# Two-layer HGRN2 and attention trunk: forget and query products moved ahead of v, attention scores taken eight heads at a time, and both groups of the recurrence in the same visits

## The chip, the cores and the metric

The kernel runs on one core of a Trainium2 chip. The metric is the time of one execution on the device in microseconds (us). A core has five engines that work beside each other: TensorE (PE in the profile, its weight loads PEld), VectorE (DVE), ScalarE (ACT), GpSimd (POOL) and SyncE (SP, which issues the loads here). Products go from SBUF through TensorE into PSUM, eight banks of 128 x 512 fp32, and only VectorE and ScalarE take them from there.

## The reference

256 tokens of width 1024 go through two layers. Each layer takes one wide projection of the normalised input, runs two mixers on parts of it, merges them through gates, and ends in a feed-forward of hidden width 2816. Cut to what matters:

```python
for l in range(2):
    h = rmsnorm(x, norm1[l])
    hq, hf, hi, hg, aq, ak, av, ga, gb = split_cols(h @ w_in[l])
    q = silu(hq)                                   # 8 heads of 128
    f = lb + (1 - lb) * sigmoid(hf)                # decay per token and channel
    k = 1 - f
    # linear recurrence with state S of 128 x 128 per head:
    #   S_t = diag(f_t) S_(t-1) + k_t v_t^T,  o_t = q_t S_t     (v = hi)
    o = hgrn2_chunked(q, k, hi, log(max(f, 1e-30)))
    y_a = (rmsnorm(o, hg_norm[l]) * silu(hg)) @ w_pa[l]
    # 16 query heads of 64 on 4 key heads, window 128, partial rope, sinks
    y_b = swa_with_sinks(rope(aq), rope(ak), av, attn_sinks[l]) @ w_pb[l]
    x = x + (sigmoid(ga) * y_a + sigmoid(gb) * y_b) @ w_o[l]
    h2 = rmsnorm(x, norm2[l])
    x = x + (silu(h2 @ w_gate[l]) * (h2 @ w_up[l])) @ w_down[l]
return rmsnorm(x, final_norm)
```

## The kernel before

**The stream.** Nearly all of TensorE's time is a stream of wide products. Each weight is split into a high part `wh` (ACT casts it, `high`) and a low part `wl` (DVE subtracts, `low`), and each product is taken three times, high by high, high by low and low by high. A unit is 128 x 1024 weights. `form_a` spends 12 products of 512 columns on one and yields after every six, `form_b` (which leaves its result transposed, tiles `pb` for hf and hq) spends eight of 512 and eight of 256 columns on one and yields after every eight. One such yield is called a step below. There are five buffers for `wh` and five for `wl` (`NW`): `used()`, called when a unit is spent, prepares the unit four further on, so the vector engines are at most about four units ahead of TensorE. SP loads weights in the order of `plan`, 1 MB at a time, into three buffers.

**The order of a layer.** `layer` goes through ak and av (one product, `akv`), aq, v (16 steps), pb (32 steps: f and q of heads 0 to 3, group 0, then of heads 4 to 7, group 1), gate (16 steps), gb, yb, gb, yb, ga, ga (8 steps each), ya, wo, and then the feed-forward. The rest of a layer are side generators: `run` counts the steps of the stream and lets each side continue after as many steps as it asked for in its last yield. What a side has TensorE do at one place is called a visit: small products between two steps of the stream. While `pe_order` is set, TensorE's instructions keep the order in which the program issues them; all others are put in order by the framework's planner, which works with its own costs.

**Attention** (`attention`, gaps `YN`, `YQ`, `YE`) starts with v. `queries` transposes q of eight heads. `attend(n)` takes the scores of four heads (tiles `qk`) into two banks tagged "at" and two tagged "hg"; DVE adds the mask and takes the maximum on the way out, ACT takes the exponentials and DVE divides. `turn(n)` transposes the weights (tiles `pt`), `values(n)` multiplies them with av (tiles `pv`), and its result is split into the pair `att` that yb reads. Counted in steps from the start of v: queries(0) at 6, scores 0 at 8 and 1 at 16, turn(0) at 20, queries(1) at 23, values 0 with scores 2 in one visit at 27, turn(1) at 31, values 1 with scores 3 at 38, turn(2) at 42, turn(3) at 53, and values 2 and 3 at 56.

**The recurrence** (`recurrence`, gaps `GAPS`) is done for each group by `decays` (sigmoids and the affine steps that make f, k and q) and `chain`, which doubles the length over which decays are multiplied together: pk (DVE), products `lb`, DVE, products `lc`, DVE, products `lv` of length 16, DVE, `lv` of length 32, DVE, `lv` of length 64 and the crossing `lx`, copies, output `o` (reads v), its norm, transposes `ot`, and the split into the pair `oT` that ya reads. Each yield of `chain` is followed by either TensorE's part or the vector part. `chain` of group 0 uses PSUM banks "hg" and the SBUF buffer "pk", group 1 "at" and "sp"; "sp" holds the scores before. Group 1 runs one stage behind group 0, so that a visit holds two different stages: lb of group 0 at step 61, lb1 with lc0 at 69, lc1 with lv16 of 0 at 82, lv16 of 1 with lv32 of 0 at 90, lv32 of 1 with lv64 and lx of 0 at 96, lv64 and lx of 1 with o of 0 at 102, o of 1 with ot of 0 at 109, ot of 1 at 115. ya begins at 112 with the half that needs group 0, and at 120 takes the half that needs group 1.

Of the kernel before, what the change touches and what calls it, by code (L numbers as in the profile page):

```python
# [15 lines left out]
P = 128  # L16
D = 1024
S = 256
# [9 lines left out]
EPS = 1e-6  # L28
MIN_F = 1e-30
NRAW, NW = 3, 5  # L30
YD, YE, YQ = 2, 3, 5
YN = (8,), (4, 3, 4), (4, 7), (4, 11)
GAPS = ((8,), (6, 7), (3, 5), (3, 3), (3, 3), (4, 3), (4, 2), (1,))
NEG = -1e30

C_HQ, C_HF, C_HI, C_HG, C_AQ, C_AK, C_GA, C_GB = 0, 1024, 2048, 3072, 4096, 5120, 5632, 6656
# [6 lines left out]
def trunk(ctx, tc, x, norm1, w_in, lb_logits, hg_norm, attn_sinks, w_pa, w_pb, w_o, norm2,  # L43
# [110 lines left out]
    plan = []  # L154
    for l in range(DEPTH):
        win = w_in[l]
        for c0 in (C_AK, C_AQ, C_AQ + 512, C_HI, C_HI + 512):
            plan += [(win, 0, 4, c0, 512), (win, 4, 4, c0, 512)]
        for g in range(2):
            for col in (C_HF, C_HQ):  # L160
                plan += [(win, 0, KT, col + 512 * g + 256 * b, 256) for b in range(2)]
        for c in range(2):
            plan += [(win, 0, 4, C_HG + 512 * c, 512), (win, 4, 4, C_HG + 512 * c, 512)]
        for c in range(2):
            plan += [(win, 0, 4, C_GB + 512 * c, 512), (win, 4, 4, C_GB + 512 * c, 512)] + a_chunk(w_pb[l], c)
        for c in range(2):
            plan += [(win, 0, 4, C_GA + 512 * c, 512), (win, 4, 4, C_GA + 512 * c, 512)]
        plan += [(w_pa[l], 4 * h, 4, 512 * c, 512) for h in range(2) for c in range(2)]
        plan += a_chunk(w_o[l], 0) + a_chunk(w_o[l], 1)
        for gi, (b0, nb) in enumerate(groups):  # L170
            for b in range(nb // 2):
                plan += [(w[l], 0, KT, (b0 + 2 * b) * P, 256) for w in (w_gate, w_up)]
            if gi:
                plan += [(w_down[l], groups[gi - 1][0], 4, 512 * c, 512) for c in range(2)]
        plan.append((w_down[l], groups[-1][0], 2, 0, D))
# [266 lines left out]
    def layer(l, n1):  # L442
# [35 lines left out]
        mix = [btile([P, D], f"mix{l}{t}") for t in range(NT)]  # L478
        gate = [btile([P, D], f"gate{l}{t}") for t in range(NT)]
        att = halves(f"att{l}")  # L480
        oT = halves(f"o{l}")
        mT = halves(f"m{l}", "rh")
        fqk = [[btile([P, 4, S], f"{n}{l}{g}", "h") for n in "fqk"] for g in range(2)]
        state = {}

        def keys():
            for t in range(NT):
# [13 lines left out]
                    T.transpose(ps[:, i * P:(i + 1) * P], aq[t][:, g * 512 + i * P:g * 512 + (i + 1) * P], ident)  # L501
                A.copy(qT[g][:, :, t * P:(t + 1) * P], ps.rearrange("p (i c) -> p i c", i=4))

        def attend(n):
            g, i0 = n // 2, 2 * (n % 2)
            s = state["sp"][:, n % 2]
            m = sm.tile([P, 4, 2, 2, 2], F32, tag="stat", name=f"stat{l}{n}", bufs=3)
            pss = [[psum(f"qk{l}{n}{t}{u}", "hg" if t else "at") for u in range(2)] for t in range(NT)]
            for t in range(NT):
                W = (t + 1) * P  # L510
                for i in range(2):
                    for u in range(2):
                        pr = slice(u * 64, u * 64 + 64)
                        T.matmul(pss[t][u][:, i * W:(i + 1) * W], qT[g][pr, i0 + i, t * P:(t + 1) * P], kT[pr, g, 0:W],
                                 start=True, stop=True)
            yield
            for t in range(NT):
                W = (t + 1) * P
                for i in range(2):
                    for u in range(2):  # L520
                        V.tensor_tensor_reduce(s[:, 2 * u + i, t * P:t * P + W], pss[t][u][:, i * W:(i + 1) * W],
                                               amask[:, 256 - W:256], op0=ALU.add, op1=ALU.max, scale=1.0,
                                               scalar=-3.0e38, accum_out=m[:, 0, t, u, i:i + 1])
            nsk = nsink.rearrange("p (l g u h) -> p l g u h", l=DEPTH, g=2, u=2)[:, l, g, :, i0:i0 + 2]
            for t in range(NT):
                V.scalar_tensor_tensor(m[:, 1, t], m[:, 0, t], -0.125, nsk, ALU.mult, ALU.min)
                V.tensor_tensor(m[:, 2, t], m[:, 1, t], nsk, ALU.subtract)
            for t in range(NT):
                for u in range(2):
                    for i in range(2):  # L530
                        sv = s[:, 2 * u + i, t * P:t * P + (t + 1) * P]
                        A.activation(sv, sv, AF.Exp, bias=m[:, 1, t, u, i:i + 1], scale=0.125,
                                     accum_out=m[:, 0, t, u, i:i + 1])
            state["exp"] = A.activation(m[:, 2], m[:, 2], AF.Exp).ins
            V.tensor_tensor(m[:, 3], m[:, 0], m[:, 2], ALU.add)
            V.reciprocal(m[:, 3], m[:, 3])
            for t in range(NT):
                for u in range(2):
                    for i in range(2):
                        sv = s[:, 2 * u + i, t * P:t * P + (t + 1) * P]  # L540
                        V.tensor_scalar(sv, sv, m[:, 3, t, u, i:i + 1], None, ALU.mult)

        def turn(n):
            s = state["sp"][:, n % 2]
            for u in range(2):
                ps = psum(f"pt{l}{n}{u}", "at")
                for i in range(2):
                    for t in range(NT):
                        T.transpose(ps[:, i * S + t * P:i * S + t * P + P], s[:, 2 * u + i, t * P:t * P + P], ident)
                A.copy(s[:, 2 * u:2 * u + 2, 0:S], ps.rearrange("p (i c) -> p i c", i=2))  # L550
            ps = psum(f"pt{l}{n}2", "hg")
            for i in range(4):
                T.transpose(ps[:, i * P:(i + 1) * P], s[:, i, 2 * P:3 * P], ident)
            A.copy(s[:, :, S:3 * P], ps.rearrange("p (i c) -> p i c", i=4))

        def values(n, bank):
            g, pT = n // 2, state["sp"][:, n % 2]
            po = psum(f"pv{l}{n}", bank)
            for u in range(2):
                vs = slice(256 + (2 * g + u) * HD, 256 + (2 * g + u + 1) * HD)  # L560
                for i in range(2):
                    o = po[i * 64:i * 64 + 64, u * S:(u + 1) * S]
                    T.matmul(o, akv[0][:, vs], pT[:, 2 * u + i, 0:S], start=True, stop=False)
                    T.matmul(o[:, P:S], akv[1][:, vs], pT[:, 2 * u + i, S:3 * P], start=False, stop=True)
            yield
            hi, lo = (a.rearrange("p (u n) c -> p n u c", u=2)[:, n % 2] for a in att[g])
            split(hi, lo, po.rearrange("p (u c) -> p u c", u=2))
# [8 lines left out]

        def attention():
            state["sp"] = sm.tile([P, 2, 4, 384], F32, tag="sp", name=f"sp{l}", bufs=1)
            for t in range(NT):
                rope(aq[t], QH, t)  # L580
            yield YQ
            queries(0)
            yield 2
            for n, gaps in enumerate(YN):
                visit = [values(n - 2, "mm")] if n > 1 else []
                together(*visit, attend(n))
                if n == 3:
                    state["last"] = True
                yield gaps[0]
                if n:  # L590
                    turn(n - 1)
                    yield gaps[1]
                if n == 1:
                    queries(1)
                    yield gaps[2]
            turn(3)
            yield YE
            together(values(2, "at"), values(3, "at"))
            yield 5

        def decays(g):
            f, q, k = fqk[g]
# [10 lines left out]
        def chain(g):  # L613
# [121 lines left out]
            for i in range(8):  # L735
                h, a = i // 2, i % 2 * P
                T.matmul(ps[0:64, i, :], k[:, h, a:a + 64], q[:, h, a + 64:a + P], start=True, stop=True)
            px = psum(f"lx{l}{g}", tag).rearrange("p (i c) -> p i c", c=P)
            for h in range(4):
                T.matmul(px[:, h, :], kx[:, h, :], qx[:, h, :], start=True, stop=True)  # L740
# [42 lines left out]
        def recurrence():  # L783
            while "last" not in state:
                yield 1
            for g in range(2):
                decays(g)
            yield YD
            chains = [chain(g) for g in range(2)]
            next(chains[0])  # L790
            yield 1
            while atd[0] is not None:
                yield 1
            for n, gaps in enumerate(GAPS):
                live = [c for g, c in enumerate(chains) if 0 <= n - g < len(GAPS) - 1]
                pe_order[0] = True
                for c in live[::-1]:
                    next(c)
                pe_order[0] = False
                for c, gap in zip(live, gaps):  # L800
                    next(c, None)
                    if n == 0:
                        next(chains[1])
                    yield gap

        yield from proj("akv", lambda t, ps: evac_scaled(akv[t], ps, rs[t]), skew=l > 0, late=None if l else rest)
# [7 lines left out]
            tables()  # L814
        finish(ksd)
        atd = start(attention(), 1)
        for c in range(2):
            yield from proj(f"v{c}", lambda t, ps: evac_scaled(v[t][:, c * 512:(c + 1) * 512], ps, rs[t]))
        for g in range(2):
            for dst in fqk[g][:2]:  # L820
                for b in range(2):
# [5 lines left out]
                        used()  # L827
                    V.tensor_tensor(dst[:, 2 * b:2 * b + 2], dst[:, 2 * b:2 * b + 2], rb, ALU.mult)
        rec = start(recurrence(), 1)

        def put_gate(c):
            def f_(t, ps):
# [331 lines left out]
```

## Time and profile before

| | |
|---|---|
| median of 3 runs | 933.36 us (932.88 to 933.45) |
| the profiled execution's own time | 933.17 us |
| its span, first to last instruction | 931.4 us |
| TensorE busy / weight loads | 923.1 us (99%) / 781.5 us |
| VectorE, ScalarE, GpSimd busy | 675.2, 540.8, 20.5 us |
| granted clock of TensorE | 0.998 of full |
| from HBM | 159.42 MB |

The span runs from the first to the last instruction; the profiled execution's own time holds 1.8 us more, before and after it. Busy times of the engines overlap. A matmul's row lasts longer than the time until the next one starts, since matmuls are pipelined; the price of a product is read from start to start.

### The profile page before, as it was taken

To read this page: it belongs to the slowest core of one execution; us is meant where nothing else is said; L and a number is where in the kernel's file an instruction comes from. 1 tells how busy PE (TensorE), PEld (TensorE's weight loads), DVE (VectorE), ACT (ScalarE), POOL (GpSimd) and SP (SyncE) were. 2 spreads that over 40 slices of the span, in tenths; PEclk is the share of its full clock that TensorE was granted. 3 is DMA by queue.
4 is the path that set the end of the run, shared out by engine and by line. 5 is a ranking of instruction groups with operands and counts; after the bars stand their busy time and mean duration, and the time that the engine had idled before them with its cause. 6 is when DMAs were issued, how large, how long until landed. Compare 5 with 4: busy or idle time off the path is not lost.

```text
span 931.4 us, 14391 instructions
## 1 busy us (share of the span) xinstructions
PE 923.1 (99%) x5726; PEld 781.5 (84%) x5726; DVE 675.2 (72%) x1171; ACT 540.8 (58%) x914; POOL 20.5 (2%) x31
## 2 busy tenths in 40 slices
PE   9999999999999999999999999999999999999997
PEld 7888888888888888888888888888888888888885
DVE  6667789975778766766865677898667777667665
ACT  6566795465456545545555867945554565555553
POOL 2000000001000000000000000000010000000000
PEclk9999999999999999999999999999999999999999
DMA  8735426644546655566465444545445565556531
GB/s 299 259 127 192 136 92 194 205 145 136 181 136 200 198 190 181 186 197 203 163 200 187 136 137 145 173 162 194 151 153 180 165 197 181 181 189 203 194 138 46
DMA packets 111395, 161.40 MB, mean 173 GB/s; under 512 B 2912, under 2 KB 64672, under 8 KB 111328
## 3 DMA queue, kind: packets, MB, share of 16 engines
q1 hardware_dynamic: 110848, 159.42, 52.5%
q8 instruction: 45, 0.74, 0.3%
q10 hardware_dynamic: 320, 0.79, 0.2%
q0 software_dynamic: 160, 0.26, 0.1%
q14 instruction: 22, 0.18, 0.1%
HBM read 159.42 MB, written 1.05 MB: 172 GB/s over the span
## 4 chain that ended last, share of the span: by engine, by line
PE 99%; DVE 0%; ACT 0%; POOL 0%; issue 0%; DVEq 0%; ACTq 0%; POOLq 0%
PE pg L57 13%; PE pu L57 13%; PE acc L57 13%; PE pb L57 10%; PE gate L57 5%; PE gb L57 5%; PE v L57 5%; PE yb L57 5%; PE wo L57 5%; PE ya L57 5%; PE ga L57 5%; PE aq L57 5%; PE akv L57 2%; PE qk L57 1%; PE pv L57 1%; PE o L57 1%
## 5 line engine op out<-in xcount | busy, mean ns | idle before, releaser
L57 DVE TENSOR_TENSOR wl<-raw,wh 128x1024 fp32r<-128x1024 f32 (+1 forms) x301 | 364.3, 1220 | 126.8 <-ACT wh L57 125.4
L57 ACT CAST wh<-raw 128x1024 fp32r<-128x1024 f32 (+1 forms) x301 | 314.5, 1050 | 168.5 <-PE acc L57 46.0
L57 PE MATMUL pu<-xx_n,wh 128*128 128x512 f32 x352 | 92.6, 393 | 0.0
L57 PE MATMUL pg<-xx_n,wh 128*128 128x512 f32 x352 | 92.1, 393 | 0.0
L57 PEld LDWEIGHTS pg<-xx_n,wh 128*128 128x128 f32 x352 | 63.2, 189 | 11.0
L57 PEld LDWEIGHTS pu<-xx_n,wh 128*128 128x128 f32 x352 | 63.1, 189 | 10.9
L57 PE MATMUL acc<-wh,ah 128*128 128x512 f32 x174 | 68.1, 391 | 0.0
L57 PE MATMUL acc<-wh,al 128*128 128x512 f32 x174 | 67.8, 390 | 0.0
L57 PE MATMUL acc<-wl,ah 128*128 128x512 f32 x174 | 67.8, 389 | 0.0
L57 PE MATMUL pb<-xx_n,wh 128*128 128x512 f32 x256 | 66.3, 396 | 0.0
L57 PEld LDWEIGHTS pb<-xx_n,wh 128*128 128x128 f32 x256 | 45.4, 189 | 8.9 <-DVE wl L57 0.7
L57 PEld LDWEIGHTS pg<-xx_n,wl 128*128 128x128 f32 x352 | 48.4, 190 | 4.1 <-ACT xx_n L57 0.6
L57 PEld LDWEIGHTS pu<-xx_n,wl 128*128 128x128 f32 x352 | 48.4, 191 | 3.6
L57 PE MATMUL pg<-xx_n,wl 128*128 128x256 f32 x352 | 50.3, 284 | 0.0
L57 PE MATMUL pu<-xx_n,wl 128*128 128x256 f32 x352 | 49.8, 283 | 0.0
L57 ACT COPY zg<-pg 128x256 f32<-128x256 f32 x44 | 16.4, 372 | 53.1 <-PE pg L57 53.1
L57 PE MATMUL gate<-wh,xx_n 128*128 128x512 f32 x128 | 41.5, 395 | 0.0
L57 ACT ACTIVATE sp<-sp,stat 128x128 f32<-128x128 f32 (+1 forms) x64 | 28.2, 442 | 22.5 <-DVE stat L57 22.5
L57 PE MATMUL gb<-wh,xx_n 128*128 128x512 f32 x128 | 41.2, 393 | 0.0
L57 PE MATMUL ga<-wh,xx_n 128*128 128x512 f32 x128 | 41.0, 394 | 0.0
L57 PE MATMUL v<-wh,xx_n 128*128 128x512 f32 x128 | 40.9, 394 | 0.0
L57 PE MATMUL aq<-wh,xx_n 128*128 128x512 f32 x128 | 40.3, 391 | 0.0
(247 smaller groups left out, 1671.2 us busy)
## 6 DMA issues: line engine op xcount, KB each, us to landing
raw<-in_w_in SPq DMA_DIRECT2D x58, 1024.0 KB, 5.2
raw<-in_w_gate SPq DMA_DIRECT2D x22, 1024.0 KB, 5.1
raw<-in_w_up SPq DMA_DIRECT2D x22, 1024.0 KB, 5.0
raw<-in_w_down SPq DMA_DIRECT2D x22, 1024.0 KB, 5.0
raw<-in_w_pb SPq DMA_DIRECT2D x8, 1024.0 KB, 5.1
raw<-in_w_pa SPq DMA_DIRECT2D x8, 1024.0 KB, 4.9
raw<-in_w_o SPq DMA_DIRECT2D x8, 1024.0 KB, 4.9
raw<-in_w_in SPq DMA_DIRECT2D x3, 512.0 KB, 7.4
```

Source lines behind the costliest of these rows:

```text
L57: ins = call(*args, **kw)
```

## The change

In `layer`, the projections of f and q (pb) come before those of v, in the order of `plan` and of the products. Attention still starts after aq, so it now runs beside pb and the first v steps.

`attend(g)` takes the scores of eight heads in one visit: the four of the first half share the "at" banks with the second half for the first token block, and their second token block goes to two "mm" banks, which the stream also uses. The exponentials of the halves follow one after the other. Scores of the third and fourth half lie in other buffers ("pk" and two new tiles tagged "r"), so that all four are kept until one visit takes all values. `turn` copies its third bank with two ACT instructions and not one.

`recurrence` calls `decays` for both groups three steps apart, starts `chain` only when attention has ended, and then lets both groups do the same stage in the same visit; `chain` has a yield more, between lv64 and lx, so that the visit of `LEV` takes lv64 of both groups and then lx of both.

Counted in steps from the start of pb, the visits are now: queries(0) at 6, queries(1) at 7, scores of eight heads at 9, turn(0) at 20, turn(1) at 24, scores of the other eight at 26, turn(2) at 37, turn(3) at 44, all values at 47; pk of group 0 at 48 and of group 1 at 51; then, each for both groups, lb at 54, lc at 66, lv16 at 78, lv32 at 88, lv64 and lx at 96, o at 102, ot at 108. v takes steps 32 to 48, gate 48 to 64, ya begins at 112 as before.

```diff
-YD, YE, YQ = 2, 3, 5
-YN = (8,), (4, 3, 4), (4, 7), (4, 11)
-GAPS = ((8,), (6, 7), (3, 5), (3, 3), (3, 3), (4, 3), (4, 2), (1,))
+YD, YE, YQ = 3, 1, 5
+YN = (6, 5, 4, 2), (6, 5, 7, 3)
+LEV = 3, 3
+GAPS = (6, 6), (6, 6), (5, 5), (4, 4), LEV, (4, 2), (1, 1)
...
-        for c0 in (C_AK, C_AQ, C_AQ + 512, C_HI, C_HI + 512):
+        for c0 in (C_AK, C_AQ, C_AQ + 512):
             plan += [(win, 0, 4, c0, 512), (win, 4, 4, c0, 512)]
         for g in range(2):
             for col in (C_HF, C_HQ):
                 plan += [(win, 0, KT, col + 512 * g + 256 * b, 256) for b in range(2)]
+        for c in range(2):
+            plan += [(win, 0, 4, C_HI + 512 * c, 512), (win, 4, 4, C_HI + 512 * c, 512)]
...
+        state = {"sr": [btile([P, 4, S], f"sr{l}{u}", "r") for u in range(2)]}
...
+        def score(n, u):
+            if n < 2:
+                return state["sp"][:, n, 2 * u:2 * u + 2]
+            return state["sq"][:, 2 * u:2 * u + 2] if n == 2 else state["sr"][u].rearrange(
+                "p a c -> p (a c)")[:, 0:768].rearrange("p (i c) -> p i c", i=2)
+
+        def attend(g):
+            t0 = [psum(f"qk{l}{g}0{u}", "at") for u in range(2)]
+            t1 = [[psum(f"qk{l}{g}1{i0}{u}", "hg" if i0 else "mm") for u in range(2)] for i0 in range(2)]
+            ms, pss = [], []
+            for i0 in range(2):
...
+                pss.append([[ps[:, i0 * S:i0 * S + S] for ps in t0], t1[i0]])
+                for t in range(NT):
...
+                            T.matmul(pss[i0][t][u][:, i * W:(i + 1) * W], qT[g][pr, 2 * i0 + i, t * P:(t + 1) * P],
+                                     kT[pr, g, 0:W], start=True, stop=True)
+            yield
+            for i0, (m, ps) in enumerate(zip(ms, pss)):
...
+                            V.tensor_tensor_reduce(score(2 * g + i0, u)[:, i, t * P:t * P + W],
...
+            for i0, m in enumerate(ms):
...
+                            A.activation(sv, sv, AF.Exp, bias=m[:, 1, t, u, i:i + 1], scale=0.125,
...
+                yield
...
-            A.copy(s[:, :, S:3 * P], ps.rearrange("p (i c) -> p i c", i=4))
+            for u in range(2):
+                A.copy(score(n, u)[:, :, S:3 * P], ps[:, u])
...
+            queries(0)
+            yield 1
+            queries(1)
             yield 2
+            for g, gaps in enumerate(YN):
+                it = attend(g)
+                together(it)
+                yield gaps[0]
+                next(it)
+                if g == 1:
                     state["last"] = True
+                yield gaps[1]
+                turn(2 * g)
+                yield gaps[2]
+                turn(2 * g + 1)
+                yield gaps[3]
+            together(*(values(n, ("at", "hg")[n % 2]) for n in range(4)))
             yield YE
...
                 T.matmul(ps[0:64, i, :], k[:, h, a:a + 64], q[:, h, a + 64:a + P], start=True, stop=True)
+            yield
             px = psum(f"lx{l}{g}", tag).rearrange("p (i c) -> p i c", c=P)
...
             for g in range(2):
                 decays(g)
-            yield YD
-            chains = [chain(g) for g in range(2)]
-            next(chains[0])
-            yield 1
+                yield YD
             while atd[0] is not None:
                 yield 1
-            for n, gaps in enumerate(GAPS):
-                live = [c for g, c in enumerate(chains) if 0 <= n - g < len(GAPS) - 1]
+            chains = [chain(g) for g in range(2)]
+            for c in chains:
+                next(c)
+                yield 3
+            for gaps in GAPS:
                 pe_order[0] = True
-                for c in live[::-1]:
-                    next(c)
+                for _ in range(1 + (gaps is LEV)):
+                    for c in chains:
+                        next(c)
                 pe_order[0] = False
-                for c, gap in zip(live, gaps):
+                for c, gap in zip(chains, gaps):
                     next(c, None)
-                    if n == 0:
-                        next(chains[1])
                     yield gap
...
         atd = start(attention(), 1)
-        for c in range(2):
-            yield from proj(f"v{c}", lambda t, ps: evac_scaled(v[t][:, c * 512:(c + 1) * 512], ps, rs[t]))
         for g in range(2):
...
         rec = start(recurrence(), 1)
+        for c in range(2):
+            yield from proj(f"v{c}", lambda t, ps: evac_scaled(v[t][:, c * 512:(c + 1) * 512], ps, rs[t]))
```

## Rows read from the trace of the kernel before

**Rows 1.** The page's first part (busy time, share of the span and instructions of each engine), and the view of waits for TensorE: who waited for whom, us in total, times, the longest.

```profile
PE 923.1 (99%) x5726; PEld 781.5 (84%) x5726; DVE 675.2 (72%) x1171; ACT 540.8 (58%) x914; POOL 20.5 (2%) x31
...
PE warm L57 <- POOL ident L57: 1.6, 1, 1.6
```

**Rows 2.** The chain that ended last, in order of time, in two stretches: start in us, us, what, how many instructions.

```profile
372.00 5.58 PE pg L57 x32
...
478.84 8.17 PE aq L57 x36
```

**Rows 3.** TensorE's timeline in the second layer around the visit of lb of group 0 and in the visit of lb of group 1 and lc of group 0: start, us, engine, line, operation, out<-in, rows*columns of the array, count.

```profile
605.01 0.39 PE L57 MATMUL gate<-wh,xx_n 128*128 128x512 f32 x1
605.33 1.31 PE L57 MATMUL lb<-pk,k 128*32 128x80 f32 x64
606.57 0.50 PE L57 MATMUL gate<-wh,xx_n 128*128 128x512 f32 x1
606.91 0.40 PE L57 MATMUL gate<-wl,xx_n 128*128 128x512 f32 x1
...
617.68 1.31 PE L57 MATMUL lb<-pk,k 128*32 128x80 f32 x64
618.81 0.86 PE L57 MATMUL lc<-p,k 128*32 128x48 f32 x64
```

**Rows 4.** The same view around three visits of attention: scores alone, values with scores, and values of two halves.

```profile
512.68 0.39 PE L57 MATMUL v<-wh,xx_n 128*128 128x512 f32 x1
513.00 1.58 PE L57 MATMUL qk<-kT,qT 64*128 64x128 f32 x16
...
514.85 0.40 PE L57 MATMUL v<-wl,xx_n 128*128 128x512 f32 x1
...
544.29 0.63 PE L57 MATMUL pb<-xx_n,wl 128*128 128x256 f32 x4
544.85 1.57 PE L57 MATMUL pv<-sp,akv 128*64 128x256 f32 x16
546.35 1.58 PE L57 MATMUL qk<-kT,qT 64*128 64x128 f32 x16
...
548.44 0.63 PE L57 MATMUL pb<-xx_n,wh 128*128 128x512 f32 x2
...
595.18 0.39 PE L57 MATMUL gate<-wh,xx_n 128*128 128x512 f32 x1
...
598.64 0.39 PE L57 MATMUL gate<-wl,xx_n 128*128 128x512 f32 x1
```

**Rows 5.** The same view at the beginning of the visit that holds lv64 and lx of group 1, and around the last transposes `ot`.

```profile
670.26 0.39 PE L57 MATMUL ga<-wh,xx_n 128*128 128x512 f32 x1
670.58 1.15 PE L57 MATMUL lv<-q,k 128*64 128x64 f32 x16
671.65 1.16 PE L57 MATMUL lx<-qx,kx 128*128 128x128 f32 x8
...
696.38 0.40 PE L57 MATMUL ya<-wh,o1l 128*128 128x512 f32 x1
...
697.72 0.39 PE L57 MATMUL ya<-wl,o1h 128*128 128x512 f32 x1
```

**Rows 6.** Windows of the second layer: v, pb, gate, and gb to the second yb. Columns: stretch, its length, busy us (and instructions) of PE, PEld, DVE, ACT, POOL, granted clock, DMA share, GB/s.

```profile
501.30:527.20 25.90, 25.90 (x137) 20.79 (x136) 17.07 (x49) 18.17 (x35) 0.00 (x0) 1.00 0.43 135
527.20:583.30 56.10, 56.10 (x365) 48.77 (x366) 42.48 (x129) 39.57 (x98) 0.00 (x0) 1.00 0.49 156
583.30:611.00 27.70, 27.70 (x206) 22.68 (x205) 24.18 (x38) 23.39 (x34) 0.00 (x0) 1.00 0.49 166
611.00:662.50 51.50, 51.50 (x601) 42.60 (x600) 46.90 (x81) 27.71 (x38) 0.00 (x0) 1.00 0.53 172
```

**Rows 7.** VectorE's timeline between the visits at 605.33 and 617.68.

```profile
605.17 1.24 DVE L57 TENSOR_TENSOR q<-pk,f 128x256 f32<-128x256 f32 x2
606.30 0.97 DVE L57 TENSOR_TENSOR pk<-pk,f 128x768 f32<-128x768 f32 x1
607.17 0.71 DVE L57 TENSOR_TENSOR f<-f 128x512 f32<-128x512 f32 x1
...
611.44 0.68 DVE L57 TENSOR_TENSOR pk<-pk,f 128x512 f32<-128x512 f32 x1
...
612.38 0.62 DVE L57 TENSOR_TENSOR pk<-pk,f 128x256 f32<-128x256 f32 x1
612.90 2.37 DVE L57 TENSOR_TENSOR wl<-raw,wh 128x1024 fp32r<-128x1024 f32 x2
615.17 1.41 DVE L57 SCALAR_TENSOR_TENSOR gate<-gate,r_n,gate 128x512 f32<-128x512 f32 x2
```

**Rows 8.** Three rows of timelines: a cast on ScalarE, a product on VectorE, and the beginning of the visit of lc of group 1 with lv16 of group 0 on TensorE.

```profile
604.08 1.05 ACT L57 CAST wh<-raw 128x1024 fp32r<-128x1024 f32 x1 [1.03 <-PE gate L57]
...
634.78 0.76 DVE L57 TENSOR_TENSOR q<-p,f 128x256 f32<-128x256 f32 x2
...
637.50 0.89 PE L57 MATMUL lc<-p,k 128*32 128x48 f32 x64
```

**Rows 9.** GpSimd's timeline in the second layer (the load that spreads the row of norms), and from the groups of instructions of VectorE between 501.3 and 583.3 the masked maximum of 256 columns: count | busy us, mean ns | idle before.

```profile
490.60 0.56 POOL L406 DMA_DIRECT2D rb_n<-row_n  x1 [1.62 <-ACT aq L57]
...
L57 DVE CUSTOM_DVE_ANT_0 sp<-qk,cf 128x256 f32<-128x256 f32 x16 | 5.8, 420 | 0.0
```

More of the change, by code (lines that the diff above doesn't have):

```diff
@@ L483, in layer @@
         fqk = [[btile([P, 4, S], f"{n}{l}{g}", "h") for n in "fqk"] for g in range(2)]
-        state = {}
         def keys():
@@ L502, in queries @@
                 A.copy(qT[g][:, :, t * P:(t + 1) * P], ps.rearrange("p (i c) -> p i c", i=4))
[L504 to L511, printed above, removed]
-                    for u in range(2):
[L513 to L519, printed above, removed]
-                    for u in range(2):
[L521 to L541, printed above, removed]
@@ new lines, in score @@
+        def score(n, u):
[8 more added lines that the diff above has]
+            for i0 in range(2):
+                ms.append(sm.tile([P, 4, 2, 2, 2], F32, tag="stat", name=f"stat{l}{2 * g + i0}", bufs=3))
+                pss.append([[ps[:, i0 * S:i0 * S + S] for ps in t0], t1[i0]])
+                for t in range(NT):
+                    W = (t + 1) * P
+                    for i in range(2):
+                        for u in range(2):
+                            pr = slice(u * 64, u * 64 + 64)
+                            T.matmul(pss[i0][t][u][:, i * W:(i + 1) * W], qT[g][pr, 2 * i0 + i, t * P:(t + 1) * P],
+                                     kT[pr, g, 0:W], start=True, stop=True)
+            yield
+            for i0, (m, ps) in enumerate(zip(ms, pss)):
+                for t in range(NT)[::-1]:
+                    W = (t + 1) * P
+                    for u in range(2):
+                        for i in range(2):
+                            V.tensor_tensor_reduce(score(2 * g + i0, u)[:, i, t * P:t * P + W],
+                                                   ps[t][u][:, i * W:(i + 1) * W], amask[:, 256 - W:256],
+                                                   op0=ALU.add, op1=ALU.max, scale=1.0, scalar=-3.0e38,
+                                                   accum_out=m[:, 0, t, u, i:i + 1])
+            for i0, m in enumerate(ms):
+                n = 2 * g + i0
+                nsk = nsink.rearrange("p (l g u h) -> p l g u h", l=DEPTH, g=2, u=2)[:, l, g, :, 2 * i0:2 * i0 + 2]
+                for t in range(NT):
+                    V.scalar_tensor_tensor(m[:, 1, t], m[:, 0, t], -0.125, nsk, ALU.mult, ALU.min)
+                    V.tensor_tensor(m[:, 2, t], m[:, 1, t], nsk, ALU.subtract)
+                for t in range(NT):
+                    for u in range(2):
+                        for i in range(2):
+                            sv = score(n, u)[:, i, t * P:t * P + (t + 1) * P]
+                            A.activation(sv, sv, AF.Exp, bias=m[:, 1, t, u, i:i + 1], scale=0.125,
+                                         accum_out=m[:, 0, t, u, i:i + 1])
+                state["exp"] = A.activation(m[:, 2], m[:, 2], AF.Exp).ins
+                V.tensor_tensor(m[:, 3], m[:, 0], m[:, 2], ALU.add)
+                V.reciprocal(m[:, 3], m[:, 3])
+                for t in range(NT):
+                    for u in range(2):
+                        for i in range(2):
+                            sv = score(n, u)[:, i, t * P:t * P + (t + 1) * P]
+                            V.tensor_scalar(sv, sv, m[:, 3, t, u, i:i + 1], None, ALU.mult)
+                yield
@@ L543, in turn @@
         def turn(n):
-            s = state["sp"][:, n % 2]
             for u in range(2):
@@ L548, in turn @@
                     for t in range(NT):
[L549 to L553, printed above, removed]
-            A.copy(s[:, :, S:3 * P], ps.rearrange("p (i c) -> p i c", i=4))
+                        T.transpose(ps[:, i * S + t * P:i * S + t * P + P], score(n, u)[:, i, t * P:t * P + P], ident)
+                A.copy(score(n, u)[:, :, 0:S], ps.rearrange("p (i c) -> p i c", i=2))
+            ps = psum(f"pt{l}{n}2", "hg").rearrange("p (u i c) -> p u i c", u=2, i=2)
+            for u in range(2):
+                for i in range(2):
+                    T.transpose(ps[:, u, i], score(n, u)[:, i, 2 * P:3 * P], ident)
+            for u in range(2):
+                A.copy(score(n, u)[:, :, S:3 * P], ps[:, u])
         def values(n, bank):
-            g, pT = n // 2, state["sp"][:, n % 2]
+            g = n // 2
             po = psum(f"pv{l}{n}", bank)
@@ L562, in values @@
                     o = po[i * 64:i * 64 + 64, u * S:(u + 1) * S]
-                    T.matmul(o, akv[0][:, vs], pT[:, 2 * u + i, 0:S], start=True, stop=False)
-                    T.matmul(o[:, P:S], akv[1][:, vs], pT[:, 2 * u + i, S:3 * P], start=False, stop=True)
+                    T.matmul(o, akv[0][:, vs], score(n, u)[:, i, 0:S], start=True, stop=False)
+                    T.matmul(o[:, P:S], akv[1][:, vs], score(n, u)[:, i, S:3 * P], start=False, stop=True)
             yield
@@ L578, in attention @@
             state["sp"] = sm.tile([P, 2, 4, 384], F32, tag="sp", name=f"sp{l}", bufs=1)
+            state["sq"] = sm.tile([P, 4, 384], F32, tag="pk", name=f"sq{l}", bufs=1)
             for t in range(NT):
@@ L582, in attention @@
             queries(0)
+            yield 1
+            queries(1)
             yield 2
[L584 to L587, printed above, removed]
-                    state["last"] = True
[L589 to L596, printed above, removed]
+            for g, gaps in enumerate(YN):
[4 more added lines that the diff above has]
+                if g == 1:
+                    state["last"] = True
+                yield gaps[1]
[4 more added lines that the diff above has]
+            together(*(values(n, ("at", "hg")[n % 2]) for n in range(4)))
             yield YE
-            together(values(2, "at"), values(3, "at"))
-            yield 5
         def decays(g):
```

## The prediction

> **What bounds the kernel now.** First the page's busy times and the waits of TensorE: 923.1 us busy in a span of 931.4, and one wait, 1.6 us at the start [rows 1]. The reader is to see that no other engine ever makes TensorE wait, so that the time is a sum of TensorE's products. Then the chain that ended last, for the price of the stream: 36 products of 512 columns in 8.17 us, 0.227 each, so that a step of six is 1.36 us; 16 of 512 and 16 of 256 in 5.58 us, which leaves 0.122 for one of 256 and makes a step of pb 1.40 us [rows 2]. The change neither adds nor removes a product. What it can change is what surrounds them: the loss at the edges of a visit, and waits that TensorE does not have now.
>
> **The price of an edge.** I take a visit's price as the time from the last stream product before it to the second one behind it, less two stream products (0.454), because a product's start is late on both sides. The visit of lb alone: 606.91 - 605.01 - 0.454 = 1.45 us. In the visit that goes on with lc, lc starts 1.13 us after lb, so lb itself is worth 1.13 and the two edges 0.32 [rows 3]. A visit of transposes has no such edge: 697.72 - 696.38 - 0.454 = 0.89 for eight, 0.11 each, which is what their columns take [rows 5]. Only visits of narrow products (32 or 64 rows or columns of the array) pay, so moving queries(1) up to one step behind queries(0) and changing the turns of the scores costs or gains nothing.
>
> **Attention's visits.** Scores alone: 514.85 - 512.68 - 0.454 = 1.72, less 0.32: four heads are worth 1.40. Two values: 598.64 - 595.18 - 0.454 = 3.01, less 0.32: 1.345 each. Values with scores: 548.44 - 544.29 less eight products of 0.122 = 3.18; less 0.32, 1.40 and 1.345 there is 0.115 left for going from one kind of narrow product to the other [rows 4]. Before, a layer has two visits of scores, two mixed and one of values: 2 x 1.72 + 2 x 3.18 + 3.01 = 12.8 us. After, two of 2.80 + 0.32 and one of 5.38 + 0.32: 11.94. Gain 0.86 us a layer.
>
> **The recurrence's visits.** Four pure narrow visits stay four (lb, lc and both short lv), 0.32 each. The two that go from lv to lx become one. That saves one entry, 670.58 - 670.26 - 0.227 = 0.09 [rows 5], and two changes of kind (lv32 to lv64, and one of two lv64 to lx). No row shows those alone; I take the 0.115 of [rows 4], the nearest, so 0.32 us a layer; the ends are 0.09 (they cost nothing) and 0.55 (twice that). The same products in the same order can't lose by it.
> The Trainium skill (TensorEngine Tiling (Array Packing), Key Properties) says that a change of tiling mode drains TensorE while a change of tile doesn't. By that rule lb to lc is free and lv to lx isn't, and the sum is the one I take, 2.4 us; if only the change that [rows 4] shows cost anything, it would be 1.9.
>
> **Sum without waits.** 0.86 + 0.32 = 1.18 a layer, 2.36 in two (1.9 to 2.8). From the profiled execution's 933.17: 930.8; that execution was 0.2 below the median, so 931.0.
>
> **What is put at nothing, and its cover.** The order of loads: all units are 1 MB and DMA is busy half the time or less [rows 6]; SP has only other loads behind them. The spread row of norms is issued on POOL's queue at 490.6 [rows 9]; its first use moves from behind v to four steps of 1.40 behind the end of aq at 501.3, still 16 us later. Four more copies a layer on ScalarE, which is busy 58% [rows 1]. Two "mm" banks given to scores: of four, one is in use and one being emptied; if they come back late, the stream waits for four masked maxima of 0.42 [rows 9], 1.7 us, but its next bank is the third and not these. The two tiles tagged "r" are freed with the values, and the `oT` that now reuse the space of `att` are written after step 108, when yb has read `att` (step 96).
>
> **What is not nothing: vector work in front of a joint visit.** Group 0's stage used to be due at one visit and group 1's at the next. Now both are due together, and TensorE's order there is fixed. The tightest place is lc. VectorE from 605.17 to 612.90 (7.73 us) did group 0's stage but for two of four products q<-pk, and three products pk of group 1 (0.87, 0.60, 0.52, by the next row's start); two q<-pk are 1.13 [rows 7]. So one group's stage is 7.73 - 1.99 + 1.13 = 6.87 us, two are 13.7. The gate's two rows take 1.32, a wl 1.13 [rows 7]. After: from group 0's lb to lc there are the other lb and the edges, 1.45 us, and 12 steps, 16.3: 17.8 us. 13.7 + 1.3 leave 2.8 us, two or three wl, while TensorE spends six units. The rest must come from the four units of lead, or from q products done before lb. It fits, with nothing to spare. Elsewhere there is room: lv16 needs only part of what has to be done by lc, again in 12 steps. The same strain is in the kernel before: VectorE is busy 46.9 of 51.5 us between gb and yb [rows 6], the wl whose cast was done at 605.13 ran at 612.90, 7.8 us late, [rows 7, 8] and TensorE still didn't wait; a q product ended at 635.54, 2.0 us ahead of its visit at 637.50 [rows 8]. So the planner uses the lead, and I take the waits as nearly nothing. A second load on the way: `decays` moves from gate, where ScalarE is busy 23.4 of 27.7 us [rows 6], into v, still behind the last exponentials, and eats into the lead with which lb is reached.
>
> **Rivals.**
> *Forecast (0.45):* waits stay under 0.2 us a layer: 930.4 to 931.5.
> *A, the gain is eaten (0.36):* at lc, or at lb behind pk of group 1 (three steps, 4.1 us, for a copy and 2.0 us of products), TensorE waits 0.3 to 2.1 us a layer; with 1 us, 931.0 + 2 = 933.0. For it: the sum above has no slack, and lead must be full at lb. Against it: the 7.8 us by which a wl was put off before.
> *B, slower (0.17):* the low parts keep their place in VectorE's list ahead of group 1's stage. Then 13.7 + 1.3 + 6 x 1.13 = 21.8 us stand against 17.8: TensorE waits 4.0 us a layer at lc, 8 in all: 939. It decides from 2.1 us a layer on (2.36 + 1.87 over two layers), which is more than four wl done in that window. Against it: [rows 7, 8], where stage work went first.
> The Trainium skill (TensorE: Matmul & The Clock Gate, the part on the array of 16 sub-arrays) says that VectorE's queue is strictly first in, first out: the list once made isn't mended on the chip. The late wl agrees, 7.8 us ready and not run; by that rule B's price is paid in full where the list is wrong.
> *C, it doesn't do what it says (0.02):* stream products that are not held in order slip between the two groups' parts, edges stay, 933.3. Against it: mixed visits ran unbroken [rows 3, 4].
>
> **How the numbers follow.** A measurement of this kernel tells about 0.2% from no change, 1.87 us: below 931.49 is faster, above 935.23 slower. Forecast: faster, 0.45. A and C: within, 0.38. B: slower, 0.17. The likeliest single time is 931.0, its own range 930.4 to 931.5. The range over all goes from 930.2 (edges at their upper end, less a little) to 935.0; it leaves out most of B.
>
> **What would show it.** TensorE's waits still at 1.6 us, and its chain as the only one. Scores in two visits a layer of some 2.8 us between starts, values in one of some 5.4, lb in one of some 2.4 before the stream resumes. No stretch of the stream over 0.23 us a product in front of lc and lb. Wrong: waits of TensorE for VectorE at lb, lc or lv, or for "mm" banks near the scores; or joint visits that cost as much as the two before, which would make the edge something other than a fixed price.

## The result and the profile after

The changed kernel takes 937.29 us (median of 4 runs, 936.84 to 938.78), the kernel before 933.4 beside it: a ratio of 1.0046 with a 95% interval of 1.0034 to 1.0059. It is slower by 3.9 us, where 931.0 was forecast and 930.2 to 935.0 allowed. Two slow executions at a lower granted clock, one of the kernel before (1315.2 us) and one of the run with the order alone (1513.95 us), are counted nowhere below.

The profiled execution took 938.78 us (span 937.0), the longest of the four. The page's busy times, and behind them the waits of TensorE of 0.6 us or more (us in total, times, the longest):

```profile
PE 923.2 (99%) x5726; PEld 782.2 (83%) x5726; DVE 674.4 (72%) x1171; ACT 540.9 (58%) x922; POOL 19.5 (2%) x31
```

```profile
PE v L58 <- DVE wl L58: 2.6, 4, 0.8
PE warm L58 <- POOL ident L58: 1.5, 1, 1.5
PE v L58 <- ACT wh L58: 1.4, 2, 0.7
...
PE pt L58 <- ACT sq L58: 0.6, 2, 0.3
```

Against [rows 1], TensorE's busy time and ScalarE's are as before; 5.5 us of waits are new. 4.6 of them are in v (`pt` are the fourth turn's transposes, which fall into v); the other 0.9 stand before the first `akv` products of the program, 6 to 9 us after its start, where the products begin no more than 0.3 us later than before. None is at lb, lc or a narrow level. The visits themselves came out as forecast. TensorE's timeline of the second layer, at the second scores and at the values:

```profile
548.61 2.89 PE L58 MATMUL qk<-kT,qT 64*128 64x128 f32 x32
551.43 1.19 PE L58 MATMUL pb<-xx_n,wh 128*128 128x512 f32 x4
...
586.59 2.87 PE L58 MATMUL pv<-sp,akv 128*64 128x256 f32 x32
589.24 1.52 PE L58 MATMUL pv<-sq,akv 128*64 128x256 f32 x16
590.54 1.52 PE L58 MATMUL pv<-sr,akv 128*64 128x256 f32 x16
592.00 0.50 PE L58 MATMUL v<-wh,xx_n 128*128 128x512 f32 x1
```

Eight heads' scores hold the stream up for 2.82 us from start to start, all values for 5.41 (forecast: some 2.8 and 5.4). So what the change was to save it saves, and something in v takes more than that. The same view where TensorE stood still in v:

```profile
571.95 0.69 PE L58 MATMUL v<-wh,xx_n 128*128 128x512 f32 x2
573.41 0.50 PE L58 MATMUL v<-wl,xx_n 128*128 128x512 f32 x1 [0.76 <-DVE wl L58]
...
580.00 0.77 PE L58 MATMUL pt<-ident,sr 128*128 128x128 f32 x5 [0.31 <-ACT sq L58]
581.48 0.73 PE L58 MATMUL v<-wh,xx_n 128*128 128x512 f32 x2 [0.71 <-ACT wh L58]
582.74 0.50 PE L58 MATMUL v<-wl,xx_n 128*128 128x512 f32 x1 [0.53 <-DVE wl L58]
```

How such rows are read: the number in brackets begins at the modelled end of the last product. From 571.95 to 573.41 are 1.46 us for two products that take 0.454 [rows 2], so 1.0 us is lost where the row says 0.76. The sum of the waits is a lower bound.

Who is late is told by the chain that ended last, between 555 and 600 (start, us, what):

```profile
555.85 1.60 ACT sq L58 x8
...
561.04 3.51 ACT sr L58 x16
...
565.88 1.28 ACT L58
567.18 1.06 ACT f L58
568.24 0.95 ACT k L58
569.19 1.31 ACT f L58 x3
...
580.48 0.95 ACT wh L58
581.46 1.24 DVE wl L58
582.74 3.92 PE v L58 x16
```

For 27 us, from the first exponential of the third half to the last late cast (`wh`) and its low part (`wl`), the chain doesn't touch TensorE: exponentials (`sq`, `sr`), a table load, decays (`f`, `k`), copies of transposes. The rows of ScalarE's timeline that begin this stretch:

```profile
548.99 1.05 ACT L58 CAST wh<-raw 128x1024 fp32r<-128x1024 f32 x1
555.85 0.40 ACT L58 ACTIVATE sq<-sq,stat 128x128 f32<-128x128 f32 x1 [5.81 <-DVE stat L58]
...
559.99 1.06 ACT L58 CAST wh<-raw 128x1024 fp32r<-128x1024 f32 x1
...
564.81 1.05 ACT L58 CAST wh<-raw 128x1024 fp32r<-128x1024 f32 x1
...
571.07 1.03 ACT L58 CAST wh<-raw 128x1024 fp32r<-128x1024 f32 x1
...
573.05 1.03 ACT L58 CAST wh<-raw 128x1024 fp32r<-128x1024 f32 x1
...
580.37 2.00 ACT L58 CAST wh<-raw 128x1024 fp32r<-128x1024 f32 x2
```

ScalarE first stands 5.81 us before an exponential that waits for 16 masked maxima on VectorE. Behind the cast at 548.99 it makes four casts up to 580.4. One cast feeds a unit, in v 12 products or 2.72 us of the stream at 0.227 each; in these 31.4 us TensorE took the products of nine units (48 in pb, 16 to a unit, and 72 in v) and stood still in between. It lived on the lead, which lasted until about 572.65, 0.76 us before the product at 573.41. That ScalarE is busy 58% of the span says nothing of this: it is an average over stages.

### The profile page after: what moved, and what is told of

The parts are those of the page before. It is cut to its first block, busy times and chain, and to the rows that moved or that the text cites. A ratio compares the mean times of both kernels' runs of the same rounds, so it can differ in the third digit from the quotient of the medians.

```text
span 937.0 us, 14410 instructions
## 1 busy us (share of the span) xinstructions
PE 923.2 (99%) x5726; PEld 782.2 (83%) x5726; DVE 674.4 (72%) x1171; ACT 540.9 (58%) x922; POOL 19.5 (2%) x31
## 4 chain that ended last, share of the span: by engine, by line
PE 91%; ACT 6%; DVE 2%; DMA 1%; issue 0%; SPq 0%; DVEq 0%; ACTq 0%
PE pg L58 13%; PE pu L58 13%; PE acc L58 13%; PE pb L58 8%; PE yb L58 5%; PE wo L58 5%; PE gate L58 5%; PE gb L58 5%; PE ga L58 5%; PE ya L58 5%; PE aq L58 5%; PE akv L58 2%; PE v L58 1%; ACT wh L58 1%; ACT f L58 1%; PE pv L58 1%
## 5 line engine op out<-in xcount | busy, mean ns | idle before, releaser
L58 PE MATMUL v<-wh,xx_n 128*128 128x512 f32 x128 | 42.8, 406 | 1.4 <-ACT wh L58 1.4
L58 PEld LDWEIGHTS acc<-wh,al 128*128 128x128 f32 x174 | 32.7, 188 | 6.8
```

Of the source, the lines that this page charges most:

```text
L58: ins = call(*args, **kw)
```

## The experiments

Two things in v were suspected: that ScalarE's list there is too long since decays joined it (theory 1), and that 16 maxima in one run make everything behind them late (theory 2). The kernel before took 933.5 us beside the first eight runs.

**Thin decays.** Most of ScalarE's work in decays is left out.

```
-                A.activation(f, f, AF.Sigmoid)
-                A.activation(k, q, AF.Sigmoid)
+                A.activation(f[:, :, 0:16], f[:, :, 0:16], AF.Sigmoid)
+            G.memset(k, 0.5)
...
-            A.activation(k, f, AF.Identity, bias=ones[:, 0:1], scale=-1.0)
+            A.activation(k[:, :, 0:16], f[:, :, 0:16], AF.Identity, bias=ones[:, 0:1], scale=-1.0)
```

> The changed kernel with ScalarE's share of decays cut to a tenth (leaves out most of the sigmoids and affine steps: 16 of 256 tokens, and k is set to a constant by GpSimd). The trace of the changed kernel has TensorE wait only in v, where ScalarE is busy without a gap from the last exponentials to turn(3) (97.8 to 120.9 us in the first layer). Theory 1, the casts of the weights stand behind ScalarE's list of exponentials, table load and decays: with some 9 us a layer less in that list the waits in v go, 930 to 931 us. Theory 2, it is the burst of eight heads (16 masked maxima on VectorE before the first exponential, 5.8 us in which ScalarE stands still): most of the waits stay, 935 or more. Theory 3, the waits are VectorE's low parts and not ScalarE's: no change, 937.

Measured 930.39 us (930.07 to 930.75), and TensorE's only wait is the 1.6 us at the start. Without waits the change is worth 3.1 us; the waits cost 937.3 - 930.4 = 6.9. That fits theory 1.

**Decays of group 1 nine steps later.**

```
-                yield YD
+                yield (12, 3)[g]
```

> The changed kernel with decays of group 1 nine steps later (step 45 and not 36); nothing is left out. Theory 1: ScalarE's 5 us for group 1 then come after the casts have caught up, so half to all of the waits in v go: 930.5 to 934; if ScalarE's list is too full anyway, they reappear in front of lb at step 54. Theory 2: the waits stay, 936 or more.

Measured 936.43 (936.07 to 937.52), a miss: the wait moved. TensorE's waits in the first fence, its timeline at lc in the second, and in the third VectorE's just ahead of lc:

```profile
PE lc L58 <- DVE p L58: 3.5, 2, 1.7
PE warm L58 <- POOL ident L58: 1.6, 1, 1.6
PE v L58 <- DVE wl L58: 1.5, 2, 0.8
```

```profile
616.05 0.89 PE L58 MATMUL lc<-p,k 128*32 128x48 f32 x64
618.67 0.89 PE L58 MATMUL lc<-p,k 128*32 128x48 f32 x64 [1.74 <-DVE p L58]
```

```profile
613.43 1.22 DVE L58 TENSOR_TENSOR wl<-raw,wh 128x1024 fp32r<-128x1024 f32 x1
...
615.71 1.23 DVE L58 TENSOR_TENSOR wl<-raw,wh 128x1024 fp32r<-128x1024 f32 x1
```

Of 4.6 us of waits in v 1.5 are left, and 3.5 stand at lc, where group 1's stage ends late, with two low parts of 1.2 us ahead of its last products. So lc has no slack to spare, as the prediction said, and decays can't simply be put off: they are squeezed between v's casts and lc.

**Maxima by halves.** The maxima of the second four heads go behind the bias of the first four.

```
-            for i0, (m, ps) in enumerate(zip(ms, pss)):
+            def maxima(i0):
+                m, ps = ms[i0], pss[i0]
...
             for i0, m in enumerate(ms):
                 n = 2 * g + i0
+                maxima(i0)
```

> The changed kernel with the masked maxima of the second four heads behind the bias of the first four on VectorE, so that the first exponentials start after 8 maxima and not 16. Theory 2: ScalarE's gap of 5.8 us shrinks to about 3.5 and the waits in v go nearly altogether, 931 to 933. Theory 1: the list behind is as long as before, ScalarE gains up to 2.2 us a layer in front of it; 933.5 to 936.

Measured 932.97 (932.66 to 933.47), better than theory 1 allowed. ScalarE stands still for 3.59 us in place of 5.81, and the casts before the decays come that much earlier. The waits in v that remain:

```profile
PE v L58 <- DVE wl L58: 1.5, 2, 0.8
PE v L58 <- ACT wh L58: 0.3, 2, 0.2
```

So both theories hold a part: 4.3 us hang on the run of 16 maxima, though work alone, taken from behind it, also suffices (thin decays). Both come down to ScalarE's time in this stage: 2.2 us a layer given back to it ahead of the exponentials (5.81 - 3.59) are worth 2.2 us a layer in the program.

**Attention's part alone**, in the old order and with the old recurrence: v ahead of pb, decays in gate, eight heads per visit.

```
-        rec = start(recurrence(), 1)
-        for c in range(2):
-            yield from proj(f"v{c}", ...)
+        for c in range(2):
+            yield from proj(f"v{c}", ...)
...
+        rec = start(recurrence(), 1)
```

> Attention's part of the change alone: eight heads per visit and all values in one, with v before pb, and the recurrence staggered by group at the steps it had before (decays at 49, first lb at 61). Edges counted from the changed kernel's trace: scores 2.98 and values 5.61 a visit against 12.8 a layer before, 1.2 us a layer: 931.0. Theory 1 expects no waits, since the last exponentials are issued at step 32 and decays at 49: 930.6 to 931.4. Theory 2 expects the burst to cost here as well: 933 or more.

Measured 930.94 (930.47 to 931.3), with no wait but the first. The 16 maxima in one run cause no wait here, although ScalarE stands still for the same 5.8 us: the decays follow later (their table load comes 14.9 us after the first exponential of the third half, not 10.0), with five casts in between and not two, and more casts stand between their parts. This beats both kernels, and puts attention's gain at 2.6 us, 1.29 a layer.

**The linear steps of decays on VectorE.** The whole computation, the maxima still in one run.

```
-                A.activation(f[:, i, :], f[:, i, :], AF.Identity, bias=lb[:, l, h:h + 1], scale=oml[:, l, h:h + 1])
-            A.activation(k, f, AF.Identity, bias=ones[:, 0:1], scale=-1.0)
+                V.tensor_scalar(f[:, i, :], f[:, i, :], oml[:, l, h:h + 1], lb[:, l, h:h + 1], ALU.mult, ALU.add)
+            V.tensor_scalar(k, f, -1.0, 1.0, ALU.mult, ALU.add)
```

> The two linear steps of decays (lower bound and slope, then k = 1 - f) go from ScalarE to VectorE; nothing else changes. ScalarE's list in v is shorter by 4 x 0.52 + 1.15 = 3.2 us a group, 6.4 us a layer; VectorE, busy 9.7 of 12.0 and 6.5 of 11.1 us there, gets some 3.5 us more. Theory 1 (ScalarE's whole list between the third half's exponentials and the last casts of v is too long, whatever stands in it): the waits of 3.6 to 5 us a layer in v all but go, 930.3 to 932. Theory 2 (the 16 maxima in one run make the exponentials and the transposes late, and that lateness alone is the wait): the exponentials start no earlier, so most of the waits stay, 934.5 to 937.

Measured 930.51 (930.35 to 930.7), ratio to before 0.9969 (0.9956 to 0.9981). The exponentials begin as late as in the changed kernel and no wait is left, so lateness alone was not the cause. Windows over v in the second layer, first of the changed kernel, then of this one (stretch, length, busy PE, PEld, DVE, ACT, POOL, granted clock, DMA share, GB/s):

```profile
559.92:571.90 11.98, 11.98 (x60) 10.07 (x59) 9.72 (x27) 11.95 (x29) 0.00 (x0) 1.00 0.19 56
571.90:583.00 11.10, 8.79 (x41) 6.36 (x41) 6.52 (x7) 11.10 (x18) 0.00 (x0) 1.00 0.38 128
583.00:593.49 10.49, 10.49 (x86) 8.71 (x86) 8.67 (x10) 10.23 (x16) 0.00 (x0) 1.00 0.80 254
```

```profile
555.02:567.00 11.98, 11.98 (x60) 10.08 (x59) 11.45 (x32) 11.95 (x27) 0.00 (x0) 1.00 0.20 60
567.00:578.10 11.10, 11.09 (x55) 8.98 (x55) 11.10 (x16) 10.78 (x18) 0.00 (x0) 1.00 0.51 157
578.10:585.46 7.36, 7.36 (x73) 6.15 (x72) 6.12 (x9) 4.80 (x8) 0.00 (x0) 1.00 1.00 362
```

ScalarE was full for 33.3 of 33.6 us. Here it is full until 578 and then has time; the stage is 30.4 us long. VectorE, the third suspect in the expectation of the thin decays, is busier here than in the changed kernel (11.45 against 9.72 us, then 11.10 against 6.52), and TensorE doesn't wait: its low parts were late because the casts were. The DMA share of 0.19 and 0.20 in the first windows is the lack of casts seen from the other side: where little is cast, little is loaded.

**Both: maxima by halves and linear steps on VectorE.**

> Both: exponentials of four heads start after eight maxima, and the two linear steps of decays are on VectorE. Theory 1: no wait is left in v, span as in the run with thin decays (928.6), 930.0 to 931.0. Theory 2: no wait either, as the exponentials are early; but if b1 stays at 934.5 to 937 and this comes to 930 to 931, the maxima are the cause and the linear steps only the rest. Rival 3 (VectorE, with 7 us more a layer before the recurrence, becomes late for the first products): waits at lb or lc of 1 us or more, 932 to 935.

Measured 929.91 (929.64 to 930.34), ratio 0.9961 (0.9948 to 0.9975): the fastest of all. The halves still give 0.6 us beside the linear steps alone, and rival 3's waits at lb or lc didn't come.

**One more sigmoid.** The opposite: the sigmoid of q is issued twice.

```
                 A.activation(f, f, AF.Sigmoid)
+                A.activation(k, q, AF.Sigmoid)
                 A.activation(k, q, AF.Sigmoid)
```

> The changed kernel with the sigmoid of q issued twice (1.04 us of ScalarE four times in the program, 4.2 us in all, the result the same). Theory 1: ScalarE has no time to spare in v, each us costs about a us: 940 to 942. Theory 2 (the lateness of the exponentials sets the waits, and behind them ScalarE has room): 937 to 938.5.

Measured 942.59 (942.35 to 944.19): 5.3 us more for 4.2 us of work. ScalarE has no time to spare in v.

**The order alone**, all else as before.

```
-        for c in range(2):
-            yield from proj(f"v{c}", ...)
         for g in range(2):
             for dst in fqk[g][:2]:
...
         rec = start(recurrence(), 1)
+        for c in range(2):
+            yield from proj(f"v{c}", ...)
```

> The kernel before with the order alone changed: the products for decays ahead of v, attention in visits of four heads and the recurrence staggered as they were. The decays then fall into v by themselves. Theory 1: they compete there with the casts as in the changed kernel, but the maxima come in runs of eight, as in the run with halves, which kept 1.5 us a layer: 935 to 937.5, waits on wh and wl in v. Theory 2 (without the run of 16 maxima the order costs nothing): 932.8 to 934.

Measured 950.28 (949.71 to 950.66), far over the expectation. The old `recurrence` issues both groups' decays in one run, and between 574.5 and 595.7 ScalarE casts no weights at all: it stands 3.2 us for the maxima and then has the last exponentials, the table load, all decays and some copies to do. First TensorE's waits, then windows (columns as above) over the second layer's end of v and beginning of gate:

```profile
PE gate L57 <- ACT wh L57: 9.4, 2, 4.7
PE gate L57 <- DVE wl L57: 1.8, 2, 0.9
```

```profile
582.00:591.00 9.00, 9.00 (x47) 7.66 (x46) 4.47 (x13) 8.97 (x14) 0.00 (x0) 1.00 0.01 2
591.00:597.00 6.00, 1.29 (x8) 0.89 (x7) 4.33 (x7) 6.00 (x10) 0.00 (x0) 0.94 0.00 0
597.00:600.00 3.00, 2.08 (x5) 1.27 (x6) 2.97 (x5) 3.00 (x6) 0.00 (x0) 0.50 0.00 0
600.00:603.00 3.00, 3.00 (x8) 2.33 (x8) 3.00 (x4) 3.00 (x5) 0.00 (x0) 0.50 0.16 19
603.00:606.00 3.00, 3.00 (x14) 2.40 (x14) 3.00 (x4) 1.66 (x3) 0.00 (x0) 0.97 0.95 345
```

In the first window nothing is loaded either (DMA share 0.01). The lead covers 17.6 us (574.5 to 592.1), then TensorE stands for 4.7 us and 0.9 more, and six us run at half the clock, worth 3: 8.6 a layer, 17.2 in two, and 16.8 were measured.

**The order, with decays in gate.** The same, but `rec = start(recurrence(), 1)` stands behind v.

> The kernel before with the products for decays ahead of v, as in b3, but the recurrence (with it decays) is started behind v, as it was started behind those products before. Theory 1 (not the order costs, but that decays fall into v, where the lead of casts is not yet rebuilt after the exponentials): decays are back in gate, and the time is that of the kernel before, 932.8 to 934.5, with no wait but the 1.6 us at the start. Rival (the order itself costs: v's casts and its scaled copies meet attention's transposes and exponentials late): waits in v or gate remain, 937 to 945.

Measured 934.38 (934.14 to 935.11), ratio 1.0013 (1.0004 to 1.0022) to 933.3 beside it. One new wait is left, 0.5 us a layer at the last values, for a copy on ScalarE. The order costs 1 us by itself; 16 of the 17 us of the run before come with the place of decays (and of the first pk copy, which starts with them).

## Why the prediction was wrong

**The step that failed** is the last one of "What is not nothing": "A second load on the way: `decays` moves from gate [...] into v, still behind the last exponentials, and eats into the lead". It was named and not priced; the sum went on with waits of nearly nothing. The effect was looked for at lb, but the lead ran out within v, some 29 us before lb at 601.75. Its price is 6.9 to 7.4 us for two layers (the changed kernel less the runs with thin decays and with both mends, the second of which has all the work). It could have been worked out as the lc step was, from [rows 6]: v before has 7.7 us in which ScalarE isn't busy (25.90 - 18.17), and two groups of decays take some 11, as their rows of after show (from the table load at 565.88 to 579.4, less two casts and a copy); the trace of before has the same, 1.3 us for the table load and 4.9 a group. That is a rough estimate, as attention's part of the stage changes too; but a surplus of 3 to 4 us had to come out of a lead of which the last exponentials, just ahead, had left about two units of four (an estimate: TensorE ran on from 565.88 to 572.65, 1.2 us of it transposes, and a unit is 2.72). In the kernel before, decays begin at 578.0, at the end of pb, and gate, which holds most of them, has 4.3 us of ScalarE to spare.

A second term stands nowhere in the prediction: the run of 16 maxima, for which ScalarE stands still 5.81 us ahead of the exponentials. Split in two it gives back 4.3 of the 6.9 us. For ScalarE in v the prediction adds up no window: it names its share of the whole span, 58%, and its share in gate.

**The edges were right, and the sum somewhat small.** Without waits the change is worth 3.1 to 3.6 us, not 2.36 (1.9 to 2.8 was allowed): attention 1.29 a layer by its own run (0.86 forecast), the recurrence 0.5 by the difference between both mends and attention alone (0.32), which also holds what the order and the place of decays do. The visits' lengths in the second layer, added up from the timelines of the kernel before and of the run with both mends, fall by 0.80 (11.84 to 11.04, attention) and 0.24 (17.32 to 17.08, recurrence), and with two and one late starts of the stream less (0.1 each) that makes 1.0 and 0.34; where the other 0.45 a layer lies stays open. The Trainium skill (TensorEngine Tiling (Array Packing), Key Properties) says that a change of tiling mode drains TensorE. The shorter visits agree with it in sign; no run separates the drain from the rest of an edge. Two readings in the prediction are loose and change nothing: a unit is half of a 1 MB load, and that 0.11 a transpose is "what their columns take" isn't in its rows (128 columns take 0.057 at the stream's price). That transposes pay no edge is borne out all the same: from start to start eight take 0.79 us and twelve 1.23 in the trace of before, 0.11 for each one more.

**lc was read right.** In the changed kernel it has no wait and next to no slack: group 1's last product p ends at 621.31, in the middle of the joint visit (TensorE's row, then VectorE's):

```profile
620.64 1.70 PE L58 MATMUL lc<-p,k 128*32 128x48 f32 x128
```

```profile
620.89 0.42 DVE L58 TENSOR_TENSOR p<-p,f 128x256 f32<-128x256 f32 x1
```

Later decays brought 1.7 us there at once, in the way of rival B, with low parts ahead of group 1's stage. There B's mechanism is real, at 1.7 in place of 4.0 us a layer, and not in the kernel that was to be predicted.

**The rivals** were all of VectorE and of the recurrence's visits. B has the sign and nearly the price (4.0 us a layer, where 3.5 to 3.7 were measured), but neither the place nor the engine: that its 939 lies near 937.3 is luck. A's 0.3 to 2.1 us a layer are too few, and its place is wrong too. I looked for the tightest place where the diff adds vector work, and not on the engine to which it adds a whole stage's work by moving it. C is out: the joint visits ran unbroken.

**What would show it** did: TensorE's waits are no longer 1.6 us. But the list named lb, lc, lv and the banks of the scores, and no wait for a cast in v.

## What to carry to other kernels

When a change moves work to another stage, take the window of that stage and add it up for each engine, casts included: an engine that is busy 58% of the span can be full for 33 us on end, and what feeds the stream (here one cast per 2.72 us) is queued behind whatever stands before it. A stage in which the lead is already half spent has little cover, so more work there costs its full length or more, as the doubled sigmoid did, and so does time in which that engine stands still there, as for the run of maxima. When such a list is too long, moving a few simple steps to an engine with room there (3.2 us a group here) was worth as much as leaving most of the stage's added work out, while postponing half of that work mostly moved the wait.

## What the runs showed that was not expected

A stall can cost more than its length, because TensorE's granted clock can fall after it. The changed kernel's first layer, windows (columns as above):

```profile
119.00:121.00 2.00, 1.15 (x4) 0.67 (x5) 1.70 (x2) 2.00 (x4) 0.00 (x0) 1.00 0.00 0
121.00:123.00 2.00, 2.00 (x7) 1.50 (x6) 1.32 (x2) 2.00 (x3) 0.00 (x0) 0.51 0.14 22
123.00:125.00 2.00, 2.00 (x7) 1.62 (x6) 1.70 (x2) 2.00 (x6) 0.00 (x0) 0.64 0.96 280
125.00:128.00 3.00, 3.00 (x29) 2.33 (x28) 2.27 (x2) 2.02 (x3) 0.00 (x0) 1.00 1.02 336
```

After some short stalls (0.3 to 0.7 us by their rows, TensorE busy 1.15 of the last 2.00 us) the clock was near 0.5 of 2.4 GHz, its 1.2 GHz level, for about 3.5 us, which costs 1.7. In the second layer of the same execution, with the same stalls, it stayed at 1.00. That execution is the longest of the four, by 1.3 to 1.9 us; what decides between the two cases is open. After the stall of 4.7 us in the run with the order alone it fell to 0.50 for some six us.
